# Attention's projections dealt out anew over 18 interleaved rounds, with new step counts and new yield points, in a three-block float32 kernel

## The chip, the core and the metric

One NeuronCore of a Trainium2 chip runs the whole program. The metric is device time in microseconds from start to end of the launch; before the change the median of three runs is 2845.41 us (2844.46 to 2849.97). The engines are PE (TensorE, matmuls), DVE (VectorE), ACT (ScalarE), POOL (GpSimd) and SP (SyncE, which only issues DMAs); each works through its own list of instructions in order.

## The reference, cut to what matters

Three residual blocks over x of 1024 tokens by 1024 features, all in float32. The change lies in the first block's stick-breaking attention and in the second block, whose two halves are an RWKV-7 time mix and a dilated window attention:

```python
def stick_breaking_attention(q, k, v):        # first block
    ...
    tail = lax.cumsum(log_one_minus, axis=3, reverse=True) - log_one_minus
    weights = masked_exp(causal, log_beta + tail)
    ...

def second_block(x, ...):
    xn = rms_norm(h, norm_w)
    p = jnp.einsum('bsd,dn->bsn', xn, w_in)                    # 1024 x 8320
    p_tm = p[..., :SHIFT_COLS]                                 # r, k, v, decay and rate columns
    p_tm = p_tm + (prev - p_tm) * mu_shift                     # prev: p_tm one token earlier
    y_rwkv = rwkv7_time_mix(p_tm, p[..., RWKV_GATE0:ATT0], ...)
    y_att = mixed_dilated_attention(p[..., ATT0:ATT_GATE0], p[..., ATT_GATE0:])
    h = h + jnp.einsum('bsm,md->bsd', jnp.concatenate([y_rwkv, y_att], axis=-1), w_out)
    return rms_norm(h, final_norm_w)

# rwkv7_time_mix, per token and head (16 heads of 64):
    sa = jnp.einsum('bhvk,bhk->bhv', state, av_t)
    state = state * w_t + sa * bv_t + v_t * k_t
    y_t = state @ r_t                                          # then a group norm, a bonus, a gate
```

## The kernel before, in words

Every projection is a dense product of float32 values split into a high and a low part (fp32r), so that each product of a 128x128 weight tile takes three matmuls (`mm3`, lines 308 to 312: high by high, low by high, high by low). A projection of 128 output features over 1024 tokens (`dense_gen`, line 314) is 2 halves x 8 contraction tiles = 16 steps of three matmuls over 512 columns, 48 matmuls in all, and yields after each step. `tok_gen` does the same for attention's values with 256 columns: also 16 yields, 96 matmuls. Dense products accumulate in the PSUM tiles called pd; their weights come by four 256 KB DMAs on SP, four casts on ACT (line 281) and four subtractions on DVE (line 282).

The order of the program is made by `interleave` (line 157). It is given Python generators, each with a stated number of steps n and a stretch (a, b) of the round, and always runs the one whose position a + (b - a) * done / n is smallest; a generator gives way wherever it yields. What it sets is the order in which instructions are written, and by it their rank: a scheduler below it then puts on each engine the first instruction in that order whose inputs it takes to be ready, so later dense matmuls already slip between the links of a chain.

The first block (`mixing1`) interleaves six rounds of projections with the mixing of the round before; `M1` holds the mixing's stated steps. Rounds 1 and 2 mix by `stick` (60 steps stated and made): per 128 queries, scores, two sigmoids on ACT, masks, a running product from the end (line 577) and a product (line 578) on DVE, then PE transposes of the result `be` (line 589) and the products with v.

The second block (`rwkv`, line 926) has 18 rounds over 16 units, a unit being two heads by 512 tokens. In round `it` it interleaves

- `rw_chain` of unit it-2: eight chunks of 64 tokens, each a chain cy (line 1169) -> R (copies, lines 1170 on DVE and 1171 on ACT) -> up (1174) -> SV (1175, 1176) -> sp (1178) -> the next state (1182), with A's product (1183) at its side; then the group norm of y (lines 1186 to 1197), transposes of y (1204) and the gate. It makes 11 + `GNY` steps, as stated;
- `rw_inverse` of unit it-1: 62 small DVE instructions, and round trips through DRAM on SP's queue;
- `rw_feat` of unit it: the decay (two tanh on ACT, a scan on DVE at line 1005, two exponentials on ACT at lines 1009 and 1010) and the products from it. 20 steps are stated, 16 made;
- dense work: `ATT[it]` of attention's 28 projection jobs (q, k, gate, and values for every other head pair), then `rw_dense`, the projections of a later unit. 32 steps are stated for `rw_dense` in rounds 0 to 15; it makes 32 in rounds 0 to 13, none in round 14 and 16 in round 15.

Jobs that `ATT` leaves over go into `attention`, as the first part of the filler `fill`, of which `AFILL[it]` steps run in attention's round `it`, beside loads of q and k (`at_load`, on ACT's queue for the first unit), scores (`at_scores`) and outputs (`at_out`). The residual's eight tiles r of 512 KB each are loaded on SP in attention's round 0.

Of the kernel before, what the change touches and what calls it, by code (L numbers as in the profile page):

```python
# [12 lines left out]
AF = mybir.ActivationFunctionType  # L13
ALU = mybir.AluOpType
# [158 lines left out]

ATT = [1, 2] * 3 + [1] * 10 + [3, 3]
G1 = [0, 5, 3, 5, 1, 7]
M1 = [60, 60, 46, 46, 78]
APLAN = [(0.0, 0.8), (0.0, 0.9), (0.0, 1.0)]
AFILL = [28, 20, 6] + [6] * 14
L3 = (0.2, 1.1)
WB = [(4,), (5, 3), (4,), (5,), (5,), (4, 3)]  # L180
MRB = 2
GNY = 4
TRM = (0.0, 0.8)
# [20 lines left out]
class Kern:  # L204
# [342 lines left out]
    def stick(self, pm, pr, q, k, v, y):  # L547

        nc = self.nc
        for i in range(NT):  # L550
# [10 lines left out]
            for h in range(2):  # L561
# [17 lines left out]
                bes.append(be)  # L579
                yield  # L580
            po = self.mm_ps()[:, :128]
            for g0 in range(0, i + 1, 4):
# [351 lines left out]
    def rwkv(self):  # L934
        nc, tc, I = self.nc, self.tc, self.I
        with tc.tile_pool(name="rw", bufs=1, reuse_waits="tile") as rw, self.psum(mx=2, iv=1, ch=1, cy=1):
# [15 lines left out]
            for it in range(18):  # L952
                gens = []
                if it >= 2:
                    gens.append((self.rw_chain(rw, U[it - 2]), 11 + GNY, *PLAN[0]))
                if 1 <= it <= 16:
                    gens.append((self.rw_inverse(rw, U[it - 1]), 37, *PLAN[1]))
                if it < 16:
                    gens.append((self.rw_feat(rw, U[it]), 20, *PLAN[2]))
                jobs = list(islice(att, ATT[it]))  # L960
                gens.append((chain(*jobs, self.rw_dense(rw, it)), 32 * (it < 16) + 16 * len(jobs), *PLAN[3]))
                interleave(gens)
# [20 lines left out]
    def rw_feat(self, rw, S):  # L983
# [20 lines left out]
        yield  # L1004
        V.tensor_tensor_scan(sg, self.c("cm"), sg, 0.0, ALU.mult, ALU.add)
        e1 = self.t(rw, [128, 8, 65], "E1")
        ei = ff("ei")
        nc.gpsimd.memset(e1[:, :, 0:1], 1.0)
        nc.scalar.activation(e1[:, :, 1:65], c8(sg), AF.Exp, scale=-cc)
        nc.scalar.activation(ei, sg, AF.Exp, scale=cc)  # L1010
        S["dc"] = dc = self.t(rw, [128, 8], "dc", bufs=3)
# [134 lines left out]
    def rw_chain(self, rw, S):  # L1146
# [16 lines left out]
        for c in range(8):  # L1163
# [8 lines left out]
            for n, s in enumerate((E, O)):  # L1172
                nc.scalar.activation(sd[s], sv[s, c, n], AF.Identity, scale=dc[s])  # L1173
            nc.tensor.matmul(up, xs[:, c], R, start=True, stop=True)
            V.tensor_copy(sv[E, c, 0], up[E])
            nc.scalar.copy(sv[O, c, 1], up[O])
            both = sv[:, c].rearrange("p n v -> p (n v)")
            nc.tensor.matmul(sp, M3[:, c].rearrange("p n k -> p (n k)"), both, start=True, stop=True)  # L1178
            for n, s in enumerate((E, O)):
# [12 lines left out]
        TT(c8(y), c8(y), bc(st[:, 0:8]), ALU.add)  # L1192
        nc.scalar.activation(sq, y, AF.Square)
        yield
        V.tensor_reduce(st[:, 8:16], c8(sq), AX.X, ALU.add)
# [53 lines left out]
    def attention(self):  # L1249
# [3 lines left out]
        with tc.tile_pool(name="po", bufs=1, reuse_waits="tile") as po:  # L1253
# [28 lines left out]
            with tc.tile_pool(name="at", bufs=1, reuse_waits="tile") as at, self.psum(**PB), \  # L1282
# [13 lines left out]
                for it in range(17):  # L1296
                    gens = [(residual(), 9, 0.1, 0.9)] if it == 0 else []
                    if it < 15:
                        gens.append((self.at_load(aqk, U[it + 1]), 4 + 2 * U[it + 1]["hf"], *ALP))
                    if it < 16:  # L1300
                        gens.append((self.at_scores(at, U[it]), 25, *APLAN[0]))
                    if it >= 1:
                        gens.append((self.at_out(at, U[it - 1]), 7 + 2 * U[it - 1]["hf"], *APLAN[1]))
                    if it == 9:
                        self.mact = macts[3] = self.act_half(1, 0)
                    if AFILL[it]:
                        gens.append((islice(fill, AFILL[it]), AFILL[it], *APLAN[2]))
                    interleave(gens)
# [446 lines left out]
```

## Time and profile before

| what | value |
| --- | --- |
| median of 3 runs | 2845.41 us (2844.46 to 2849.97) |
| the profiled execution: its own time | 2842.42 us |
| the profiled execution: span, first to last instruction | 2840.6 us |
| mean granted clock of TensorE, as a share of full speed | 0.986 |
| busy: PE, PEld (weight loads), DVE, ACT, POOL | 96%, 80%, 62%, 41%, 10% |
| rounds 1 to 17 of the RWKV part | about 1071 to 2005 us of the span |
| the stick rounds | about 70 to 410 us |

The profile's waits name whom an engine sat idle for. A view by stretches gives each engine's busy time and the granted clock in a window. Granted clock 1.00 is the upper of TensorE's two levels, 2.4 GHz, and 0.50 the lower, 1.2 GHz; a value between is a mix of both over the stretch. Matmuls are pipelined, so the busy time of one (0.39 us) is longer than its share of the stream.

### The profile page before, as it was taken

What the parts mean: (1) busy time and instruction counts of PE and PEld (TensorE: products, weight loads), DVE (VectorE), ACT (ScalarE), POOL (GpSimd) and SP (SyncE); (2) the same over time, 40 slices, a digit from 0 to 9 for tenths busy, and PEclk for the clock granted to TensorE, in tenths of its full rate; (3) what the DMA queues carried; (4) which work ended last, traced back from release to release, by engine and by line L of the source; (5) the groups of instructions that cost most, each with busy time, mean ns of one, the idle gap of its engine ahead of it and who ended that gap; (6) DMA issues with size and microseconds to landing.
All of it is one profiled execution on the core that took longest, in us unless ns stands there. A gap on an engine that the chain in (4) does not pass through costs nothing. (4 is left out here: it accounts for less than half of the span.)

```text
span 2840.6 us, 50116 instructions
## 1 busy us (share of the span) xinstructions
PE 2732.7 (96%) x18984; PEld 2277.3 (80%) x18984; DVE 1762.3 (62%) x4655; ACT 1174.7 (41%) x2808; POOL 275.5 (10%) x370
## 2 busy tenths in 40 slices
PE   9999999999998999999999999989999999999999
PEld 7778787777798787778877778768889989978887
DVE  4665533433867567787787877765466676644354
ACT  4433323223324324444445444444465666442232
POOL 0000000000213100010011100100011211000100
PEclk9999999999999999999999999989999999999999
DMA  3121111114753322222222222222754553331132
GB/s 124 45 68 45 56 65 38 57 57 148 226 191 115 98 85 66 72 74 69 78 66 79 69 72 75 68 66 73 209 181 143 165 161 109 132 118 66 48 121 97
DMA packets 215265, 276.63 MB, mean 97 GB/s; under 512 B 70112, under 2 KB 105712, under 8 KB 214896
## 3 DMA queue, kind: packets, MB, share of 16 engines
q1 hardware_dynamic: 187024, 220.99, 25.4%
q10 hardware_dynamic: 28000, 52.44, 5.1%
q8 instruction: 149, 2.44, 0.4%
q14 instruction: 92, 0.75, 0.1%
HBM read 213.58 MB, written 59.77 MB: 96 GB/s over the span
## 5 line engine op out<-in xcount | busy, mean ns | idle before, releaser
L310 PE MATMUL pd<-aH,wh 128*128 128x512 f32 (+1 forms) x1824 | 758.5, 416 | 12.4 <-ACT aH L305 5.9
L312 PE MATMUL pd<-aH,wl 128*128 128x512 f32 (+1 forms) x1824 | 735.1, 403 | 2.2 <-DVE wl L282 2.2
L311 PE MATMUL pd<-aL,wh 128*128 128x512 f32 (+1 forms) x1824 | 731.2, 401 | 0.0
L282 DVE TENSOR_TENSOR wl<-wraw,wh 128x512 fp32r<-128x512 f32 (+1 forms) x429 | 305.0, 716 | 303.1 <-ACT wh L281 293.5
L281 ACT CAST wh<-wraw 128x512 fp32r<-128x512 f32 (+1 forms) x429 | 260.4, 611 | 433.8 <-PE pd L311 214.3
L310 PEld LDWEIGHTS pd<-aH,wh 128*128 128x128 f32 (+1 forms) x1824 | 345.8, 190 | 85.2 <-issue 14.4
L312 PEld LDWEIGHTS pd<-aH,wl 128*128 128x128 f32 (+1 forms) x1824 | 345.3, 189 | 72.6 <-DVE wl L282 4.5
L311 PEld LDWEIGHTS pd<-aL,wh 128*128 128x128 f32 (+1 forms) x1824 | 346.5, 190 | 57.9 <-DVE aL L306 0.4
L310 PE MATMUL pd<-wh,aH 128*128 128x256 f32 x960 | 283.1, 296 | 2.7 <-ACT wh L281 2.2
L311 PE MATMUL pd<-wl,aH 128*128 128x256 f32 x960 | 273.7, 286 | 0.9 <-DVE wl L282 0.9
L312 PE MATMUL pd<-wh,aL 128*128 128x256 f32 x960 | 272.1, 286 | 1.4 <-DVE aL L306 1.2
L310 PEld LDWEIGHTS pd<-wh,aH 128*128 128x128 f32 x960 | 183.4, 192 | 7.7 <-ACT wh L281 3.4
L311 PEld LDWEIGHTS pd<-wl,aH 128*128 128x128 f32 x960 | 183.8, 192 | 4.1 <-DVE wl L282 1.8
L312 PEld LDWEIGHTS pd<-wh,aL 128*128 128x128 f32 x960 | 183.3, 192 | 2.7 <-DVE aL L306 2.3
L1447 ACT ACTIVATE S<-S,anm 128x256 f32<-128x256 f32 (+1 forms) x256 | 118.0, 463 | 22.5 <-DVE anm L1440 19.5
L1173 ACT ACTIVATE sd<-SV,dc 64x64 f32<-64x64 f32 x256 | 88.4, 345 | 83.6 <-DVE SV L1182 78.4
L1111 DVE TENSOR_TENSOR Xt<-At,X 128x60 f32<-128x60 f32 (+24 forms) x496 | 106.4, 214 | 11.1
L1113 DVE TENSOR_TENSOR X<-X,Xt 128x60 f32<-128x60 f32 (+24 forms) x496 | 104.7, 211 | 12.2
L1398 DVE CUSTOM_DVE_ANT_0 S<-sc,cf 128x256 f32<-128x256 f32 (+1 forms) x256 | 86.1, 377 | 31.3 <-PE sc L1395 21.7
L1394 PE MATMUL sc<-kk,qq 128*128 128x256 f32 (+1 forms) x256 | 90.5, 369 | 4.6 <-DVE kk L1369 3.6
L1169 PEld LDWEIGHTS cy<-SV,M 128*128 128x128 f32 x512 | 81.1, 193 | 16.2 <-DVE SV L1182 4.1
L1182 DVE SCALAR_TENSOR_TENSOR SV<-ch,dc,sd 64x64 f32<-64x64 f32 x240 | 67.9, 283 | 30.6 <-PE ch L1178 24.2
(376 smaller groups left out, 4857.2 us busy)
## 6 DMA issues: line engine op xcount, KB each, us to landing
wraw<-in_w2fm SPq DMA_DIRECT2D x122, 256.0 KB, 2.7
wraw<-in_w1fm SPq DMA_DIRECT2D x80, 256.0 KB, 2.6
qkr<-qkg SPq DMA_DIRECT2D x152, 128.0 KB, 2.8
wraw<-in_w2out SPq DMA_DIRECT2D x64, 256.0 KB, 3.4
sgd<-s ACTq DMA_DIRECT2D x48, 256.0 KB, 2.0
sgt<-sgd SPq DMA_DIRECT2D x48, 256.0 KB, 3.6
qkg<-ast ACTq DMA_DIRECT2D x42, 256.0 KB, 2.0
wraw<-in_w3fm SPq DMA_DIRECT2D x38, 256.0 KB, 2.6
```

What stands on the lines that cost most here:

```text
L281: nc.scalar.copy(h, raw)
L282: nc.vector.tensor_tensor(l, raw, h.bitcast(F32), ALU.subtract)
L310: mm(ps, lh, rh, start=start, stop=False)
L311: mm(ps, lh, rl, start=False, stop=False)
L312: mm(ps, ll, rh, start=False, stop=stop)
L1111: eng.tensor_tensor(tmp[:, :M, :n], At[:, j:j + 1, j + 1:32].to_broadcast([128, M, n]), X[:, :M, j:j + 1].to_broadcast([128, M, n]), ALU.mult)
L1113: eng.tensor_tensor(X[:, :M, j + 1:32], X[:, :M, j + 1:32], tmp[:, :M, :n], ALU.add)
L1169: nc.tensor.matmul(xy[:, c, n], M1[:, c, n], sv[:, c, n], start=c % 4 == 0 and n == 0, stop=False, skip_group_check=True)
L1173: nc.scalar.activation(sd[s], sv[s, c, n], AF.Identity, scale=dc[s])
L1394: mm(o, q, k, start=i == 0, stop=False, skip_group_check=True)
L1398: red = lambda o, x, mk, acc: V.tensor_tensor_reduce(o, x, mk, 1.0, -3e38, ALU.add, ALU.max, acc)
L1447: nc.scalar.activation(x, x, AF.Exp, bias=nm[:, n, h, t:t + 1], accum_out=l[:, n, h, t:t + 1])
```

## The change

Numbers that set the order change, four generators get more yield points, and the scan and the exponentials of `rw_feat` are done in two halves of 256 tokens. No other instruction is added or taken away.

- `ATT`: per round before 1 2 1 2 1 2 1 1 1 1 1 1 1 1 1 1 3 3, now 1 2 1 2 1 2 1 0 1 1 0 1 1 1 3 2 2 2. The sum falls from 25 to 24: one more job (48 matmuls) goes to attention's filler, and `AFILL` starts 34, 24, 12 in place of 28, 20, 6.
- The dense steps stated per round become those made (32 up to round 13, 0 in round 14, 16 in round 15). The chain is stated as 30 + `GNY` with `GNY` 8 and makes 28 + `GNY`; `rw_feat` is stated as 22 and makes 20.
- `stick` yields 1 + i // 3 times more before its transposes of query tile i, 15 times in all, so it makes 75 steps; `M1` still states 60.
- `ASTART`: the scores of attention's first unit are spread over 0.4 to 0.95 of their round in place of 0 to 0.8.

```diff
--- before.py
+++ after.py
@@ -171,15 +171,16 @@
             live.remove(x)
 
 
-ATT = [1, 2] * 3 + [1] * 10 + [3, 3]
+ATT = [1, 2] * 3 + [1, 0, 1, 1, 0, 1, 1, 1, 3, 2, 2, 2]
 G1 = [0, 5, 3, 5, 1, 7]
 M1 = [60, 60, 46, 46, 78]
+ASTART = (0.4, 0.95)
 APLAN = [(0.0, 0.8), (0.0, 0.9), (0.0, 1.0)]
-AFILL = [28, 20, 6] + [6] * 14
+AFILL = [34, 24, 12] + [6] * 14
 L3 = (0.2, 1.1)
 WB = [(4,), (5, 3), (4,), (5,), (5,), (4, 3)]
 MRB = 2
-GNY = 4
+GNY = 8
 TRM = (0.0, 0.8)
 YD = 0
 LNP = 4
@@ -577,6 +578,8 @@
                 nc.vector.tensor_tensor_scan(omr, omr, omr, 1.0, ALU.mult, ALU.min)
                 nc.vector.tensor_tensor(be[:, :W], be[:, :W], om[:, 1:W + 1], ALU.mult)
                 bes.append(be)
+                yield
+            for _ in range(1 + i // 3):
                 yield
             po = self.mm_ps()[:, :128]
             for g0 in range(0, i + 1, 4):
@@ -952,13 +955,13 @@
             for it in range(18):
                 gens = []
                 if it >= 2:
-                    gens.append((self.rw_chain(rw, U[it - 2]), 11 + GNY, *PLAN[0]))
+                    gens.append((self.rw_chain(rw, U[it - 2]), 30 + GNY, *PLAN[0]))
                 if 1 <= it <= 16:
                     gens.append((self.rw_inverse(rw, U[it - 1]), 37, *PLAN[1]))
                 if it < 16:
-                    gens.append((self.rw_feat(rw, U[it]), 20, *PLAN[2]))
+                    gens.append((self.rw_feat(rw, U[it]), 22, *PLAN[2]))
                 jobs = list(islice(att, ATT[it]))
-                gens.append((chain(*jobs, self.rw_dense(rw, it)), 32 * (it < 16) + 16 * len(jobs), *PLAN[3]))
+                gens.append((chain(*jobs, self.rw_dense(rw, it)), 32 * (it < 14) + 16 * (it == 15) + 16 * len(jobs), *PLAN[3]))
                 interleave(gens)
             self.late_jobs = list(att)
         self.rk_pool.__exit__(None, None, None)
@@ -1002,12 +1005,17 @@
         nc.scalar.activation(ta, aps, AF.Tanh, bias=self.ha0[:, p:p + 1], scale=0.5)
         nc.gpsimd.tensor_scalar(sg, sg, 0.5, 0.5, ALU.mult, ALU.add)
         yield
-        V.tensor_tensor_scan(sg, self.c("cm"), sg, 0.0, ALU.mult, ALU.add)
         e1 = self.t(rw, [128, 8, 65], "E1")
         ei = ff("ei")
         nc.gpsimd.memset(e1[:, :, 0:1], 1.0)
-        nc.scalar.activation(e1[:, :, 1:65], c8(sg), AF.Exp, scale=-cc)
-        nc.scalar.activation(ei, sg, AF.Exp, scale=cc)
+        halves = [(slice(256 * n, 256 * n + 256), slice(4 * n, 4 * n + 4)) for n in range(2)]
+        for tk, cs in halves:
+            V.tensor_tensor_scan(sg[:, tk], self.c("cm")[:, 0:256], sg[:, tk], 0.0, ALU.mult, ALU.add)
+            yield
+        for tk, cs in halves:
+            nc.scalar.activation(e1[:, cs, 1:65], c8(sg)[:, cs], AF.Exp, scale=-cc)
+            nc.scalar.activation(ei[:, tk], sg[:, tk], AF.Exp, scale=cc)
+            yield
         S["dc"] = dc = self.t(rw, [128, 8], "dc", bufs=3)
         nc.gpsimd.tensor_copy(dc, e1[:, :, 64])
         yield
@@ -1171,10 +1179,12 @@
             nc.scalar.copy(R[O], xy[O, c, 1])
             for n, s in enumerate((E, O)):
                 nc.scalar.activation(sd[s], sv[s, c, n], AF.Identity, scale=dc[s])
+            yield
             nc.tensor.matmul(up, xs[:, c], R, start=True, stop=True)
             V.tensor_copy(sv[E, c, 0], up[E])
             nc.scalar.copy(sv[O, c, 1], up[O])
             both = sv[:, c].rearrange("p n v -> p (n v)")
+            yield
             nc.tensor.matmul(sp, M3[:, c].rearrange("p n k -> p (n k)"), both, start=True, stop=True)
             for n, s in enumerate((E, O)):
                 if not (hf == 1 and c == 7):
@@ -1191,6 +1201,7 @@
         V.tensor_scalar(st[:, 0:8], st[:, 0:8], -1.0 / 64, None, ALU.mult)
         TT(c8(y), c8(y), bc(st[:, 0:8]), ALU.add)
         nc.scalar.activation(sq, y, AF.Square)
+        yield
         yield
         V.tensor_reduce(st[:, 8:16], c8(sq), AX.X, ALU.add)
         self.rsqrt(rw, st[:, 16:24], st[:, 8:16], 1.0 / 64, 64e-5)
@@ -1298,7 +1309,7 @@
                     if it < 15:
                         gens.append((self.at_load(aqk, U[it + 1]), 4 + 2 * U[it + 1]["hf"], *ALP))
                     if it < 16:
-                        gens.append((self.at_scores(at, U[it]), 25, *APLAN[0]))
+                        gens.append((self.at_scores(at, U[it]), 25, *(APLAN[0] if it else ASTART)))
                     if it >= 1:
                         gens.append((self.at_out(at, U[it - 1]), 7 + 2 * U[it - 1]["hf"], *APLAN[1]))
                     if it == 9:
```

Round 15 on PE: the last chunks of unit 13's chain. In the file before, cy, up, sp and A's product are L1169, L1174, L1178 and L1183, in the changed one L1177, L1183, L1188 and L1193; L1066 and now L1074 are products of `rw_feat`, L311 to L313 dense matmuls. Before:

```order
L1183 MATMUL cy_18936<-SV_1575_9416,A_18087 128x128
L1169 MATMUL cy_18936<-SV_1575_9416,M_3065_18085 128x64 x2
L1174 MATMUL ch_19275<-R_19278,XS_1573_9414 128x64
L1178 MATMUL ch_19276<-SV_1575_9416,M_3103_18343 128x128
L1183 MATMUL cy_18936<-SV_1575_9416,A_18087 128x128
L1169 MATMUL cy_18936<-SV_1575_9416,M_3065_18085 128x64 x2
L1174 MATMUL ch_19352<-R_19355,XS_1573_9414 128x64
L1178 MATMUL ch_19353<-SV_1575_9416,M_3103_18343 128x128
L1183 MATMUL cy_18936<-SV_1575_9416,A_18087 128x128
L1169 MATMUL cy_19478<-SV_1574_9415,M_3175_18718 128x64 x2
L1066 MATMUL mx_19299<-M_3261_19191,At_19192 128x128 x4
```

Now, in the last chunk of the same unit:

```order
L1177 MATMUL cy_18981<-SV_1575_9416,M_3039_17880 128x64 x2
L1074 MATMUL mx_19437<-M_3269_19286,At_19287 128x128 x4
L312 MATMUL pd_19406<-aL_1099_7118,wh_19247 128x512
L313 MATMUL pd_19406<-aH_1098_7117,wl_19248 128x512
L1074 MATMUL mx_19453<-M_3269_19286,At_19287 128x128 x2
L1183 MATMUL ch_19427<-R_19430,XS_1573_9414 128x64
L1074 MATMUL mx_19453<-M_3269_19286,At_19287 128x128 x2
L311 MATMUL pd_19406<-aH_1098_7117,wh_19247 128x512
L312 MATMUL pd_19406<-aL_1099_7118,wh_19247 128x512
L313 MATMUL pd_19406<-aH_1098_7117,wl_19248 128x512
L311 MATMUL pd_19406<-aH_1098_7117,wh_19247 128x512
L1188 MATMUL ch_19428<-SV_1575_9416,M_3065_18084 128x128
```

Before, three chunks run with nothing between their links, and the feature products come after them; now feature products and two to four dense matmuls stand between the links.

ACT in round 3, around the exponentials: E and ei are their outputs, R is the chain's copy. Before:

```order
L1001 ACTIVATE fs_11317<-mx_11284,hw_1504_9143 128x512
L1002 ACTIVATE ta_11318<-mx_11285,ha_1505_9145 128x512
L1009 ACTIVATE E_1899_11338<-fs_11317 128x8x64
L1171 COPY R_11296<-cy_11212 64x64
L1010 ACTIVATE ei_11339<-fs_11317 128x512
L1016 ACTIVATE fs_11378<-rkv_1654_9826,pf 128x512
L1176 COPY SV_1575_9416<-ch_11293 64x64
```

Now:

```order
L1004 ACTIVATE fs_11319<-mx_11289,hw_1504_9143 128x512
L1005 ACTIVATE ta_11320<-mx_11290,ha_1505_9145 128x512
L1181 ACTIVATE sd_11309<-SV_1575_9416,dc_10081 64x64 x2
L1016 ACTIVATE E_1899_11340<-fs_11319 128x4x64
L1017 ACTIVATE ei_11341<-fs_11319 128x256
L1016 ACTIVATE E_1899_11340<-fs_11319 128x4x64
L1017 ACTIVATE ei_11341<-fs_11319 128x256
L1179 COPY R_11310<-cy_11221 64x64
L1024 ACTIVATE fs_11461<-rkv_1653_9823,pf 128x512
```

R stood behind one whole exponential; here it stands behind four halves. In the 14 rounds that have feature and chain together it stands behind two halves in four, three in five and four in five.

SP at the start of attention: cf are constants, ag and vn gate and values of the first unit, r the residual's tiles, qkr raw q and k of the second unit. Before:

```order
L227 DMA cf_20582<-in_c 128x784
L1382 DMA ag_20591<-qkg 128x512
L1384 DMA vn_20592<-vd 128x4x128
L1293 DMA r_3473_20543<-hd 128x1024
L1293 DMA r_3474_20544<-hd 128x1024
L1415 DMA vn_20674<-vd 128x4x128
L1293 DMA r_3475_20545<-hd 128x1024
L1293 DMA r_3476_20546<-hd 128x1024
L1293 DMA r_3469_20539<-hd 128x1024
L1354 DMA qkr_20584<-qkg 64x512 x2
```

Now:

```order
L228 DMA cf_20560<-in_c 128x784
L1304 DMA r_3463_20521<-hd 128x1024
L1304 DMA r_3464_20522<-hd 128x1024
L1304 DMA r_3465_20523<-hd 128x1024
L1304 DMA r_3466_20524<-hd 128x1024
L1393 DMA ag_20646<-qkg 128x512
L1395 DMA vn_20647<-vd 128x4x128
L1304 DMA r_3459_20517<-hd 128x1024
L1304 DMA r_3460_20518<-hd 128x1024
L1365 DMA qkr_20562<-qkg 64x512 x2
L1365 DMA qkr_20602<-qkg 64x512 x2
```

Four of the eight r loads moved ahead of the first unit's gate and values, and six, no longer five, stand ahead of the second unit's q and k.

## Rows read from the trace of the kernel before

**Rows 1.** The page: busy time by engine; granted clock in 40 slices.
```profile
PE 2732.7 (96%) x18984; PEld 2277.3 (80%) x18984; DVE 1762.3 (62%) x4655; ACT 1174.7 (41%) x2808; POOL 275.5 (10%) x370
...
PEclk9999999999999999999999999989999999999999
```

**Rows 2.** Stretches of rounds; us, busy by engine, PEclk, DMA share, GB/s.
```profile
1674.50:1732.30 57.80, 55.34 (x356) 43.10 (x356) 44.85 (x141) 28.29 (x69) 6.86 (x11) 1.00 0.23 69
1800.00:1851.40 51.40, 47.96 (x320) 36.64 (x320) 42.88 (x126) 24.85 (x63) 7.00 (x12) 0.99 0.25 78
1851.40:1906.70 55.30, 43.83 (x274) 35.58 (x273) 42.59 (x133) 23.68 (x60) 3.73 (x5) 0.81 0.18 46
1906.70:1956.80 50.10, 48.85 (x297) 39.34 (x297) 28.59 (x112) 23.12 (x60) 2.68 (x3) 0.95 0.31 98
```

**Rows 3.** The same stretches, line 310 alone (one dense matmul in three).
```profile
1674.50:1732.30 57.80, 19.98 (x48) 9.11 (x48) 1.00 0.23 69
1800.00:1851.40 51.40, 15.05 (x35) 6.67 (x35) 0.99 0.25 78
1851.40:1906.70 55.30, 8.85 (x22) 4.25 (x21) 0.81 0.18 46
```

**Rows 4.** PE's timeline, first and last of 48 dense matmuls; start, duration in us.
```profile
1303.62 0.47 PE L310 MATMUL pd<-aH,wh 128*128 128x512 f32 x1
...
1314.38 0.39 PE L312 MATMUL pd<-aH,wl 128*128 128x512 f32 x1
```

**Rows 5.** PE's waits in 60:420, 1060:1800 (two rows), 2002:2100; total, times, longest.
```profile
PE mx L589 <- DVE be L578: 10.7, 11, 1.3
...
PE ch L1174 <- ACT R L1171: 14.9, 15, 1.7
PE ch L1204 <- DVE tt L1197: 2.2, 3, 1.2
...
PE sc L1394 <- DVE kk L1369: 3.6, 2, 2.3
```

**Rows 6.** PE's timeline in round 15; idle before and releaser in brackets.
```profile
1885.66 0.64 PE L1183 MATMUL cy<-SV,A 128*128 128x128 f32 x2
...
1899.66 0.90 PE L1204 MATMUL ch<-cf,tt 128*128 128x128 f32 x3 [2.57 <-DVE tt L1197]
```

**Rows 7.** Timelines of DVE and ACT in round 14, scan, exponential and R.
```profile
1806.80 1.22 DVE L1005 TENSOR_TENSOR_SCAN fs<-cf,fs 128x512 f32<-128x512 f32 x1
...
1808.05 0.63 ACT L1009 ACTIVATE E<-fs 128x512 f32<-128x512 f32 x1 [1.72 <-DVE fs L1005]
1808.71 0.21 ACT L1171 COPY R<-cy 64x64 f32<-64x64 f32 x1
```

**Rows 8.** ACT's groups by shape; busy, mean ns of one.
```profile
L1447 ACT ACTIVATE S<-S,anm 128x256 f32<-128x256 f32 x176 | 87.0, 496 | 12.4 <-DVE anm L1440 12.4
...
L1009 ACT ACTIVATE E<-fs 128x512 f32<-128x512 f32 x16 | 10.1, 632 | 21.4 <-DVE fs L1005 21.3
```

**Rows 9.** PE's timeline, a stick tile's last scores and its transposes.
```profile
174.92 0.63 PE L568 MATMUL mx<-f,q 128*128 128x512 f32 x2
...
181.11 0.95 PE L589 MATMUL mx<-cf,be 128*128 128x128 f32 x7 [1.31 <-DVE be L578]
```

**Rows 10.** PE's timeline in round 12, last product of the chain and y's transposes.
```profile
1715.23 0.39 PE L1183 MATMUL cy<-SV,A 128*128 128x128 f32 x2
...
1728.00 0.66 PE L1204 MATMUL ch<-cf,tt 128*128 128x128 f32 x4 [0.75 <-DVE tt L1197]
```

**Rows 11.** Stretches at the start of attention (as rows 2); landing of r's loads.
```profile
2010.00:2020.00 10.00, 8.13 (x36) 6.38 (x34) 0.96 (x2) 1.84 (x3) 0.00 (x0) 1.00 1.01 290
2020.00:2030.00 10.00, 8.30 (x36) 6.80 (x37) 4.39 (x14) 2.88 (x5) 0.00 (x0) 0.83 1.01 291
...
DMA to landing us min/median/max: 3.9/5.9/7.1
```

## The prediction, made before the changed kernel was run

> **What bounds the kernel now.** I read the page first: PE is busy for 96% of the span [rows 1], so no other engine is the bound as a whole, and as the change removes no matmul it can only win time in which PE stands still or runs slowly. The page's row of granted clock shows where to look, one slice under 0.9; a matmul's busy time is not its share of the stream, so I did not take the 96% for the limit. The second view is by stretches, cut where the RWKV rounds begin on PE (the transposes of v, line 1101). Round 12 is 57.8 us at clock 1.00; round 15 is 55.3 us with PE busy for only 43.8 of them and a granted clock of 0.81; round 16 has 0.95 [rows 2]. The third view counts dense work in them by line 310, one dense matmul in three: 48, then 35 in round 14 and 22 in round 15 [rows 3]. So round 15 is almost as long as round 12 with less than half of its dense work: the stated 32 steps that `rw_dense` does not make had used up the filler early. The last view is PE's waits by releaser: stick's transposes wait 10.7 us in 11 places, the chain's up product 14.9 us in 15, y's transposes 2.2 us, and attention's first scores 3.6 us [rows 5].
>
> **The change part by part.** A dense matmul costs 10.76 us / 47 = 0.229 us in the stream [rows 4].
>
> Round 15. Its rest beside dense work is 55.3 - 66 x 0.229 = 40.2 us; round 12's is 57.8 - 144 x 0.229 = 24.8 us [rows 2, 3]. The order now gives round 15 all 144 dense matmuls, placed between the links that stood bare. If its rest becomes that of round 12, the gain is **15.4 us**. What hides the chain is then this filler; without it the next to be late are y's transposes, which came 14.0 us after the chain's last product there, 2.57 us of it idle [rows 6].
>
> Round 14. Rest 51.4 - 105 x 0.229 = 27.4 us, so **2.6 us** to gain by the same step [rows 2, 3]. Round 16: half speed for 10% of 50.1 us makes work of 2.5 us cost 5; without the hole before it, **2.5 us** [rows 2].
>
> The light rounds. Rounds 7 and 10 lose a job each and have 105 and 107 dense matmuls in the new order. The nearest row is round 14 before, with 105: **-2.6 us each, -5.2** [rows 2, 3]. The bounds are nothing, if the new points of giving way cover it, and -15.4 each, if they go the way of round 15; I take round 14, whose count is the same.
>
> The group norm's tail. In round 12 y's transposes came 12.8 us after the last product and still waited 0.75 us [rows 10]. By counts from the new order at 0.229 us a dense and some 0.1 us a small matmul, an estimate, the work between the two is 6.0, 7.7 and 7.5 us in three rounds (7, 10 and 11) and 9.8 or more in the others with features, where the least was 9.2 before round 14. Beyond what the light rounds are charged I take **-3 us**; bounds 0 and -15, as three tails of 12.8 us would have it.
>
> The scan in halves. Before, the scan takes 1.22 us, E follows for 0.63 and R is done 0.21 after [rows 7], and up waits for it about 1 us a round. A half scan is an estimate of 0.61 us. A half exponential lies between half of 0.632 us and the 0.496 us of ACT's nearest shape of 256 columns [rows 8]; I take 0.40. Where R stands behind two halves it comes about 0.4 us sooner, behind three it comes at the same time, behind four 0.4 us later: nearly nothing over the 14 rounds. But the order now writes the previous chunk's sp and A and one dense matmul more behind the feature's first products and ahead of this up, some 0.45 us of work in most rounds: 14 x 0.45 = 6 us, of which I take **4**. The bounds are +14.9, every wait gone, and -6, 15 waits longer by 0.4. The Trainium skill ("VectorE: DVE Perf Modes", section on the TRN2 errata) says that operations from SBUF pay a fixed cost each on ScalarE and VectorE and advises tiles of at least 512 elements, which speaks against halves. Its formula gives an estimated 0.40 us for a half exponential, which fits between the rows; by that rule the halves cost ACT 0.17 us each, and the sum stays as it is because ACT is not the bound.
>
> Stick. In query tile 7 the second head's transposes start 6.2 us after the last scores, 1.31 us of it idle [rows 9]. Before, 12 to 15 dense matmuls (2.7 to 3.4 us) stood there; now 18 to 30 do (4.1 to 6.9 us) in tiles 0 to 6, which covers the waits. But 75 steps run against 60 stated, so the dense steps run out early: in tile 7 only 14 follow the last scores, and the last products get less between them. Of 10.7 us [rows 5] I leave about 6 standing or new: **+5**; bounds +10.7 and +2.
>
> Attention's start. One job moves here (48 x 0.229 = 11.0 us of PE work, four weight loads of 256 KB on SP, two stores on ACT's queue); PE's sum is unchanged. Of dense work after y's transposes there were 69 matmuls of 512 columns, 15.8 us; now 45 of these and 36 of 256 columns, an estimate of 14.6 us, precede the first scores, so these wait longer. The DMA engines are full there, share 1.01 and 290 GB/s [rows 11], and four r loads, 2.1 MB or 7.2 us at that rate, moved ahead. SP's waiting r loads also hold the gate and values queued behind them, which are needed only later. Against that stands more filler once the scores run. I take **-1 us**; bounds -15, those 7.2 us waited for at half speed, and +8, all waits and half speed gone.
>
> Nothing else costs: the added scan and exponentials lie beside PE's work, and 15 further idle points in stick and four more before y's transposes issue nothing. In rounds 14 and 15 the added jobs put eight weight loads each between the inverse's round trips on SP, as in rounds 2 to 6 before, at clock 1.00.
>
> **Sum.** 15.4 + 2.6 + 2.5 - 5.2 - 3 + 4 + 5 - 1 = 20.3 us off the profiled execution's 2842.4, that is 2822.1. The median of the runs lies 3.0 us above that execution (2845.4), so I predict **2825.1 us**.
>
> **The rivals.** *Light rounds become holes.* DVE is busy for 42.9 of round 14's 51.4 us and 44.9 of round 12's 57.8 [rows 2]; if rounds 7 and 10 fall into waiting and half speed as round 15 did, each loses 15.4 and not 2.6: 2825.1 + 25.6 = **2850.7**, no change. For: the cover of y's transposes falls to 6.0 and 7.7 us there. Against: round 14 with the same count kept clock 0.99. Chance 0.13.
>
> *The tail is slower than its cover in all rounds* (the slower side). Place: y's transposes, with everything behind them on PE. The covers counted from the new order for rounds 2 to 15 are 10.8, 14.8, 11.0, 14.8, 10.7, 6.0, 12.2, 12.8, 7.7, 7.5, 9.9, 9.8, 12.2 and 11.3 us. If the tail always needs the 14.0 us of round 15 [rows 6], they fall short by 46.1 in all; less 2.2 waited before [rows 5] and 8.2 charged above, that is 35.7: **2860.8**. At 13 us it is 2848.8, so it decides from some 13.2 us. For: the 12.8 us with a wait of round 12 [rows 10]. Against: only three such waits stand in 12 rounds, though the same count gives covers of 9.2 to 11.6 us in six of them. The Trainium skill ("TensorE: Matmul & The Clock Gate", section on HAM oscillation) describes waits that recur in each loop pass and halve the clock each time; the 0.81 of round 15 agrees [rows 2], and by that rule the price would rise further. Chance 0.07.
>
> *Attention's first scores wait for r.* The bound of -15 in place of -1: **2839.1**. Chance 0.10.
>
> *The halves don't free R* (the change does not do there what it says): -6 in place of +4, **2835.1**. Chance 0.08.
>
> **How the numbers follow.** My forecast has 0.62, within 2806 (all waits of up and stick gone, nothing lost in the light rounds) and about 2836. A measurement of this kernel tells about 0.2% from no change, here 5.7 us. Faster by more than that (below 2839.7): the forecast 0.62, the halves 0.08, half of the r rival 0.05 and 0.03 of a partial light-round loss, 0.78. Within 0.2%: the rest of the r rival 0.05, light rounds 0.07 and the tail's low end 0.01, 0.13. Slower: light rounds 0.03, the tail 0.06, 0.09. The range 2806 to 2843 leaves out the tail, 0.10 of the light rounds and about 0.03 below.
>
> **What would show it.** Right: round 15 at clock 1.00 and 57 us with 144 dense matmuls; waits of stick's transposes under 5 us in sum; up's waits still there, 8 to 14 us in sum; rounds 7 and 10 at 47 to 52 us. Wrong: granted clock under 0.95 in round 7 or 10, y's transposes waiting over 15 us in sum between rounds 2 and 15, or over 8 us ahead of attention's first scores.

## The result and the profile after

The changed kernel takes 2816.27 us in the median (2809.37 to 2818.79), the kernel before 2847.69 (2844.46 to 2849.99) beside it: ratio 0.9885, 95% interval 0.9867 to 0.9904. That is 1.15% faster, clear of the noise of the runs, inside the range (2806 to 2843) and 8.8 us below the forecast of 2825.1. The profiled execution of the changed kernel took 2815.63 us, its span is 2813.8; that is 26.8 us less span than before, where the sum of the prediction said 20.3.

The page of the changed kernel, busy time and granted clock, as [rows 1]:

```profile
PE 2719.9 (97%) x18984; PEld 2270.6 (81%) x18984; DVE 1748.2 (62%) x4671; ACT 1177.5 (42%) x2840; POOL 274.1 (10%) x370
...
PEclk9999999999999999999999999999999999999999
```

The slice under 0.9 is gone. Stretches of the changed kernel, cut as in [rows 2] at the transposes of v (now line 1109): rounds 15 and 16 (its first 50 us), then the light rounds 7 and 10, which have no job of attention:

```profile
1824.00:1879.80 55.80, 54.88 (x356) 43.80 (x355) 43.91 (x139) 27.65 (x69) 4.30 (x6) 1.00 0.29 86
1879.80:1929.80 50.00, 48.79 (x318) 38.68 (x318) 32.15 (x124) 24.99 (x69) 2.67 (x3) 1.00 0.28 86
1377.60:1425.40 47.80, 46.89 (x318) 36.27 (x317) 42.88 (x138) 24.34 (x64) 4.92 (x9) 1.00 0.21 60
1538.70:1586.90 48.20, 47.55 (x319) 37.08 (x318) 42.37 (x141) 24.50 (x65) 5.50 (x11) 1.00 0.22 62
```

The same, line 311 alone (one dense matmul in three, as [rows 3]), round 15 and the light rounds:

```profile
1824.00:1879.80 55.80, 20.20 (x48) 9.14 (x48) 1.00 0.29 86
...
1377.60:1425.40 47.80, 14.68 (x35) 6.64 (x35) 1.00 0.21 60
1538.70:1586.90 48.20, 15.35 (x36) 6.84 (x36) 1.00 0.22 62
```

Round 15 is as long as before (55.8 against 55.3 us) and does 144 dense matmuls in place of 66, at clock 1.00 in place of 0.81. The light rounds keep the full clock too.

PE's waits of the changed kernel; total, times, longest, as [rows 5]: stick (60:420); rounds 2 to 16 (1060:1960, two rows; 1071.6 us, which the table of the kernel before gives as the start of round 1, is that of round 2); around attention's start (1960:2100):

```profile
PE mx L592 <- DVE be L579: 4.6, 5, 1.1
...
PE ch L1215 <- DVE tt L1208: 10.5, 7, 2.1
PE ch L1183 <- ACT R L1179: 4.9, 10, 1.1
...
PE sc L1405 <- DVE kk L1380: 8.2, 2, 6.8
```

Stick's transposes (L592) wait 4.6 us where they waited 10.7. The rows of rounds 2 to 16 reach to 1960, those of before to 1800; to 1800 the up product (L1183) waits 4.6 us where it was 14.9, and y's transposes (L1215) went the other way, from 2.2 to 9.3. Over all of 1060:1960 up fell from 17.6 to 4.9 us and y's transposes rose from 7.8, round 15 among them, to 10.5; the rows of the kernel before there:

```profile
PE ch L1174 <- ACT R L1171: 17.6, 18, 1.7
PE ch L1204 <- DVE tt L1197: 7.8, 6, 2.6
```

One hole is new: 6.8 us ahead of attention's first scores, which now wait 8.2 us in two waits where they waited 3.6.

The sums of waits leave out matmuls that run slowly, and the lengths of rounds move with the jobs, so I add one measure that has neither fault. For every matmul I take the time from the start of the one before it on PE, less the median of that for its line and shape in the kernel before, and sum it over a stretch: **excess**, the time in which PE stood or went slowly, however much dense work was moved in or out. In us, one profile each:

```
                               before  after   e2   e5   e9  e10  e11  e12
opening and stick                27.1   20.1 28.4 20.7 19.1 16.5 20.6 16.3
first block's rest to round 1    94.9   95.9 95.0 95.8 96.4 93.0 95.4 95.0
rounds 2 to 6                    13.1    7.9 14.2 23.7 12.5  9.5  8.2  8.2
rounds 7 to 13                   20.6   22.5 25.4 26.9 23.6 11.4 16.6 16.7
rounds 14 to 16                  28.4    4.3  5.8  8.3  5.7 13.1  4.2  4.0
to attention's last scores        8.9   13.7  8.1 14.1  7.0 22.0  7.6 13.1
all behind                       12.8   14.8 13.1 13.1 11.9 13.1 12.4 10.9
```

Before to after: 24.1 us won in rounds 14 to 16, 7.0 in opening and stick (6.4 of it in stick), 5.2 in rounds 2 to 6; 1.9 lost in rounds 7 to 13, 4.8 in attention, 3.0 in the two other rows. That is 26.6 of the 26.8 us. How far one profile can be trusted is shown by kernels that give PE the same order in the rounds: the changed one, e3, e6, e7 and e8 lie between 29.7 and 32.7 us over rounds 2 to 13. The runs behind the names come now; each stands beside runs of the kernel before of its own, and the ratio is to those.

### The profile page after: what moved, and what is told of

The parts are those of the page before. It is cut to its first block, busy times and chain, and to the rows that moved or that the text cites. A ratio compares the mean times of both kernels' runs of the same rounds, so it can differ in the third digit from the quotient of the medians.

```text
span 2813.8 us, 50166 instructions
## 1 busy us (share of the span) xinstructions
PE 2719.9 (97%) x18984; PEld 2270.6 (81%) x18984; DVE 1748.2 (62%) x4671; ACT 1177.5 (42%) x2840; POOL 274.1 (10%) x370
## 4 chain that ended last, share of the span: by engine, by line
PE 43%; DVE 5%; ACT 3%; issue 3%; DMA 2%; POOL 1%; ACTq 0%; SPq 0%; DVEq 0%; POOLq 0%
PE pd L311 8%; PE pd L312 8%; PE pd L313 8%; PE po L1483 2%; PE mx L311 2%; PE mx L312 2%; PE tr L1493 2%; PE mx L313 2%; PE sc L1405 1%; PE sc L1406 1%; PE mx L1074 1%; PE cy L1177 1%; PE ch L1188 1%; DVE wl L283 1%; PE ch L1183 1%
## 5 line engine op out<-in xcount | busy, mean ns | idle before, releaser
L311 PE MATMUL pd<-aH,wh 128*128 128x512 f32 (+1 forms) x1824 | 760.9, 417 | 12.3 <-ACT aH L306 5.9
L313 PE MATMUL pd<-aH,wl 128*128 128x512 f32 (+1 forms) x1824 | 730.3, 401 | 2.2 <-DVE wl L283 2.2
L311 PEld LDWEIGHTS pd<-aH,wh 128*128 128x128 f32 (+1 forms) x1824 | 345.6, 189 | 76.0 <-issue 6.1
L313 PEld LDWEIGHTS pd<-aH,wl 128*128 128x128 f32 (+1 forms) x1824 | 344.7, 189 | 74.6 <-DVE wl L283 3.6
L312 PEld LDWEIGHTS pd<-aL,wh 128*128 128x128 f32 (+1 forms) x1824 | 346.0, 190 | 55.8 <-DVE aL L307 0.4
L311 PE MATMUL pd<-wh,aH 128*128 128x256 f32 x960 | 281.9, 295 | 5.0 <-ACT wh L282 2.6
L313 PE MATMUL pd<-wh,aL 128*128 128x256 f32 x960 | 271.1, 285 | 0.3 <-DVE aL L307 0.3
L311 PEld LDWEIGHTS pd<-wh,aH 128*128 128x128 f32 x960 | 182.8, 191 | 8.7 <-ACT wh L282 3.7
L313 PEld LDWEIGHTS pd<-wh,aL 128*128 128x128 f32 x960 | 183.0, 191 | 1.4 <-DVE aL L307 0.8
L1177 PEld LDWEIGHTS cy<-SV,M 128*128 128x128 f32 x512 | 81.5, 189 | 23.4 <-DVE SV L1192 11.3
L1406 PE MATMUL sc<-kk,ql 128*128 128x256 f32 (+1 forms) x256 | 86.9, 351 | 0.0
```

The source lines that it names most:

```text
L311: mm(ps, lh, rh, start=start, stop=False)
L312: mm(ps, lh, rl, start=False, stop=False)
L313: mm(ps, ll, rh, start=False, stop=stop)
L1177: nc.tensor.matmul(xy[:, c, n], M1[:, c, n], sv[:, c, n], start=c % 4 == 0 and n == 0, stop=False, skip_group_check=True)
L1406: mm(o, ql, k, start=False, stop=i == len(args) - 1, skip_group_check=True)
```

## Experiments

The theory: the dealing out wins rounds 14 to 16 and loses a little in the light rounds; the points of giving way win in stick and in the chain.

**e1, true step counts alone** (on the kernel before):

```diff
-                gens.append((chain(*jobs, self.rw_dense(rw, it)), 32 * (it < 16) + 16 * len(jobs), *PLAN[3]))
+                gens.append((chain(*jobs, self.rw_dense(rw, it)), 32 * (it < 14) + 16 * (it == 15) + 16 * len(jobs), *PLAN[3]))
```

> The kernel before with the true step counts of the dense generator alone (32 only up to round 13, 16 in round 15); the jobs stay where they were. Theory 1: round 15 needs both, steps spread over the round and more of them. The 66 dense matmuls now stand between the links, so its 20.2 us of PE time above the usual spacing falls to about 8 to 12 us, with waits left over: about 2838 us, granted clock in round 15 0.9 or more. Rival: the false count was the whole fault, round 15 keeps under 3 us above the usual spacing: about 2826 us. Other rival: it is the jobs alone, and nothing changes: 2845 to 2850 us.

Measured: 2844.58 us beside 2845.12, ratio 1.0004 (0.9991 to 1.0017): the last case, nothing. Round 15 of this kernel, all engines and then line 310 alone:

```profile
1849.10:1902.60 53.50, 40.92 (x274) 33.65 (x273) 39.22 (x129) 21.68 (x58) 3.29 (x4) 0.83 0.18 49
...
1849.10:1902.60 53.50, 9.25 (x22) 4.18 (x22) 0.83 0.18 49
```

Still 66 dense matmuls, still clock 0.83; the excess of the round falls from 20.2 to 17.3 us and round 16 pays that back with 3.4. The statement of 32 steps too many was not what left round 15 bare. With 66 dense matmuls in it the hole stays, by the false counts and by the true ones.

**e2, the whole dealing out without any point** (on the kernel before: `ATT`, counts, `ASTART`, `AFILL`).

> The kernel before with the whole dealing out (table of jobs, true counts, attention's start and fill), without any new point of giving way in stick, in the features and in the chain. Theory 1: rounds 14 to 16 gain their 24 us as in the changed kernel, the light rounds 7 and 10 lose about 4 us each for want of cover ahead of y's transposes, attention's start loses 5: about 2837 us, y's transposes waiting 10 us or more in sum in rounds 2 to 13. Rival: the light rounds are free by themselves, as rounds 7 and 10 were 0.8 and 1.9 us better in the changed kernel: about 2828 us. Other rival: without the points they fall into half speed: 2845 us or more.

Measured: 2831.58 us, ratio 0.9948 (0.9929 to 0.9967), so 13.5 us of the gain. Rounds 14 to 16 win 22.6 us, rounds 2 to 13 lose 5.9 (39.6 against 33.7). Attention's start loses nothing here (8.1 against 8.9), and the clock of the light rounds 7 and 10 is 0.99 and 1.00. Theory 1 held in rounds 14 to 16; the total lies between it and its rival, 5.4 us under the one and 3.6 over the other, since attention's start was free, and y's transposes wait 6.3 us in 6 places where 10 us or more were expected.

Two things belong to this. The run has jobs and true counts together; the jobs with the false counts were not run, so e1 and e2 show that the counts alone do nothing, and not that they are of no use beside the jobs. And `tok_gen` makes 8 x 8 x 3 = 192 matmuls of 256 columns for a job of values, not the 96 given at the start. Such a job moved from round 13 to round 14, which now has 288 dense matmuls, 192 of them of that kind.

**e3 and e8, stick's points taken out of the changed kernel.** The first edit took more than it said, the point after each head that was always there as well; the second is stick as before:

```diff
 # e8
                 bes.append(be)
-                yield
-            for _ in range(1 + i // 3):
                 yield
```

> The changed kernel without stick's new points of giving way. Theory 1: the 6.4 us won in stick go back, its transposes wait 9 to 11 us again in 10 or more places: about 2822.5 us. Rival: that stretch was better for other reasons, or what is lost there is won behind it: 2816 us, the same as the changed kernel.

> The changed kernel with stick as it was before (one point after each head, 60 steps run and 60 stated). The run without any point there showed more than was asked, since it also took the one that was always there. Theory 1: the points added are worth what the two profiles differ in there, 6.4 us: waits of stick's transposes 10 to 11 us in 11 places, about 2822.5 us. Rival: stick gains nothing that is not lost behind it: 2816 us.

Measured: e3 2825.67 us (ratio 0.9928, 0.9911 to 0.9945), with stick's transposes waiting 13.8 us in 18 places; e8 2823.04 us (0.9915, 0.9895 to 0.9934), with 10.7 us in 11 places as before and 28.0 us of excess in opening and stick where the changed kernel has 20.1. With no point, one and the new ones, the transposes wait 13.8, 10.7 and 4.6 us; the new points are worth some 7 us of the total (6.8 by the medians, 8.5 by the ratios).

**e4, whole scan and exponentials**, four points left at their place:

```diff
...
-        for tk, cs in halves:
-            V.tensor_tensor_scan(sg[:, tk], self.c("cm")[:, 0:256], sg[:, tk], 0.0, ALU.mult, ALU.add)
-            yield
+        V.tensor_tensor_scan(sg, self.c("cm"), sg, 0.0, ALU.mult, ALU.add)
+        yield
...
```

> The changed kernel with scan and exponentials whole again, and four points of giving way left at their place. Theory 1: the up product waits less because the chain gives way ahead of it, and not because R is freed by halves: its waits stay at 4 to 7 us in sum, about 2816 us. Rival: the halves free R: up's waits go back to 10 us or more, about 2823 us.

Measured: 2817.12 us, ratio 0.99 (0.9875 to 0.9925), no different from the changed kernel; up waits 7.0 us in 13 places. The halves take 2.1 us of waits from up (4.9 with them) and nothing that shows from the time.

**e5, e9 and e11: how the chain is spread.** Three edits of the changed kernel:

```diff
 # e5 and e9: the two points ahead of up and sp taken out
-            yield
             nc.tensor.matmul(up, xs[:, c], R, start=True, stop=True)
-            yield
             nc.tensor.matmul(sp, M3[:, c].rearrange("p n k -> p (n k)"), both, start=True, stop=True)
 # e5: stated 14 + GNY, GNY = 8    e9: stated 12 + GNY, GNY = 1
 # e11: the points stay, stated 30 + GNY
-GNY = 8
+GNY = 12
```

> The changed kernel without the two points at which the chain gives way ahead of its up and sp products (true count 16 lower). Theory 1: these points, and not the halves, took up's waits from 14.9 to 4.6 us: they go back to 10 us or more in 12 places or more, rounds 2 to 6 lose the 6 us won there: about 2823 us. Rival: the dealing out won it, since up waited only 10.3 us in 14 places with the dealing out alone, and the points add nothing: 2816 us, up's waits 5 to 10 us.

> The changed kernel without the two points ahead of up and sp, and with one idle point instead of eight ahead of y's transposes, stated 13: the chain's products are then spread over 0.61 of a round (8 of 13 steps), as in the changed kernel (24 of 38, 0.63). Without the points and with eight idle ones it was 8 of 22, 0.36, and 2832.6 us. Theory 2: it is the pace, how much dense work stands between one chunk and the next, that the stated counts set; 2816 to 2820 us, waits of the inverse's products and of M1's gone again. Rival (theory 1 as it was): the points themselves, which split the dense work of a chunk in three parts, are needed: up waits 10 us or more in sum, 2825 us or more.

> The changed kernel with twelve idle points instead of eight ahead of y's transposes, stated 42. Theory: the tail of the group norm is what still waits in the rounds (10.5 us in 7 places); four points more put about a tenth of a round more dense work ahead of the transposes: these waits fall under 4 us, up's and sp's rise by 2 to 4 since the products are drawn closer (24 of 42 steps): about 2813 us. Rival: what the tail wins the products lose in full, as where the pace was 0.36 of a round: 2816 to 2820 us.

Measured: e5 2832.62 us (0.9937, 0.9917 to 0.9958), e9 2814.82 (0.9897, 0.987 to 0.9925), e11 2803.05 (0.9854, 0.9831 to 0.9878). PE's waits in 1060:1960, of e5, e9 and e11 in turn:

```profile
PE iv L1140 <- DVE Xt L1137: 7.4, 6, 1.9
PE ch L1182 <- ACT R L1179: 3.4, 10, 0.4
PE mx L1074 <- DVE At L1064: 3.3, 4, 2.1
```

```profile
PE ch L1182 <- ACT R L1179: 10.4, 13, 1.5
PE ch L1213 <- DVE tt L1206: 5.7, 8, 1.1
```

```profile
PE ch L1183 <- ACT R L1179: 8.3, 10, 1.4
PE ch L1215 <- DVE tt L1208: 1.0, 2, 0.8
```

e5 came out slow, and not in the way expected: up waits less than ever, the inverse's products (L1140) and the M1 products (L1074) wait instead. (Its profile is of the longest of its five executions, 2839.56 us where the median is 2832.62, so its column of excess is too high rather than too low.) By stated steps the eight chunks are then done in 8 of 22, 0.36 of the round (before 8 of 15, 0.53; changed 24 of 38, 0.63); this share I call the pace. e9 gives the pace back (8 of 13, 0.61) and not the points: the time is that of the changed kernel, the waits for the inverse are gone, and up's return to 10.4 us. So both sides were partly right. The pace is what e5 had lost; the points do take up's waits away, 36.1 us of excess in rounds 2 to 13 without them and 30.4 with them, but 6.7 us less excess in attention hides that in e9's total. e11 puts work back ahead of y's transposes: they wait 1.0 us in place of 10.5, up 8.3 in place of 4.9, rounds 2 to 13 fall to 24.8 us, and the time lies under both cases expected. Between the last product of the chain and these transposes stood 5 of 15 steps before (0.33 of a round), 10 of 38 in the changed kernel (0.26) and 14 of 42 in e11 (0.33 again). So the changed step count had spread the products at the cost of the tail's cover, and e11 gives that back.

**e6 and e7: attention's start.** e6 has the old `AFILL` and scores from 0.0 to 0.8; e7:

```diff
-gens = [(residual(), 9, 0.1, 0.9)] if it == 0 else []
+gens = [(residual(), 9, 0.9, 1.5)] if it == 0 else []
```

> The changed kernel with attention's first unit from 0.0 to 0.8 and the fill of 28, 20 and 6 as before. Theory 1: the hole of 6.8 us ahead of the first scores comes from r's four loads, which here go behind more of the first unit's own loads; waits for kk fall to 2 to 5 us, but the late job then runs later and no time is won behind: 2812 to 2816 us. Rival: the hole is the shorter filler after the last transposes of y, and the old start, with less filler ahead of the scores, makes it longer: 2820 us or more.

> The changed kernel with the eight loads of r stated from 0.9 to 1.5 of attention's first round, so that they go behind the first unit's loads. Theory 1: the first scores wait for q and k, which share the DMA engines with four loads of r (2.1 MB); without these kk comes 4 us sooner, waits for kk under 3 us in sum, attention's first stretch 13.9 to about 9 us above the usual spacing: about 2811 us. Rival: q and k come late because of what ScalarE's own queue issues and when: the wait stays over 6 us, 2816 us.

Measured: e6 2822.79 us (0.9911, 0.989 to 0.9932), e7 2814.71 (0.9884, 0.9862 to 0.9907). e6 missed both ways: the hole stays (6.0 us) and is not longer, as the rival had it; and the loss is behind attention, 20.3 us of excess in place of 14.8, with 203 more dense matmuls left for after the last scores. e7 shortens the hole to 4.5 us and wins nothing that shows. What the rest of the hole waits for stands on ScalarE's timeline of the changed kernel (ACTq is an issue of DMAs on its queue):

```profile
1965.67 0.62 ACT L282 CAST wh<-wraw 128x512 fp32r<-128x512 f32 x1 [3.13 <-DMA wraw<-in_w2fm]
...
1966.54 3.39 ACTq L1365 DMA_DIRECT2D qkr<-qkg  x4
...
1975.15 0.62 ACT L1369 CAST qq<-qkr 128x512 fp32r<-128x512 f32 x1 [4.58 <-DMA qkr<-qkg]
```

The first unit's loads are issued only behind two casts, which wait 3.13 us for a late job's weights, and then take until 1975.15. With r out of the way (e7) the same wait of the cast qq is 2.64 us, from an issue at 1962.21 to 1968.07. So r costs about 2.3 us of the 6.8.

For the rest the order on ScalarE's queue was not changed by an edit of its own, but two runs from above differ in it. e2 and e9 have the same jobs, the same start of attention and four loads of r ahead of the first unit's gate as well, and their first scores wait hardly more than before:

```profile
PE sc L1395 <- DVE kk L1370: 2.4, 1, 2.4
PE sc L1403 <- DVE kk L1378: 2.1, 1, 2.1
```

On their ScalarE the issue stands behind two casts of this job and not four, and by the profile neither of the two waits for weights. From y's last transposes to the cast kk it takes 17.2 and 17.4 us there, 17.2 in the kernel before and 20.6 in the changed kernel. So the new hole came neither with the dealing out nor with r's place alone, but with the order on ScalarE that the chain's new steps leave at the end of round 17.

**e10, no light rounds, and 75 stated steps in stick** (far apart, read by stretch):

```diff
-ATT = [1, 2] * 3 + [1, 0, 1, 1, 0, 1, 1, 1, 3, 2, 2, 2]
+ATT = [1, 2] * 3 + [1, 1, 1, 1, 1, 1, 1, 1, 2, 2, 2, 1]
...
-M1 = [60, 60, 46, 46, 78]
+M1 = [75, 75, 46, 46, 78]
```

> The changed kernel with two edits in stretches that lie far apart: no light rounds (one job in each of rounds 6 to 13, two in 14 to 16, one in 17), and stick's stated steps 75, as many as run. To be read by stretch. Jobs: by the forecast's price the light rounds cost 5.2 + 3 us, which come back in rounds 7 to 11; rounds 14 and 15 have two jobs where they had three and two, and by the run with the true counts alone (17.3 us above the usual spacing with one job) round 15 keeps its cover, round 14 loses 2 us or less: together 5 us won. Rival: light rounds cost nothing, rounds 7 to 13 stay within 2 us of the changed kernel and 14 to 16 lose up to 5. Stick: dense work that reaches the last tiles covers the 4.6 us that still wait there: 2 to 4 us won; rival: it is spread thinner, the earlier tiles wait, none won. In sum 2808 us, by the rivals 2821 us.

Measured: 2817.32 us (0.9899, 0.9876 to 0.9922). Rounds 7 to 13 win 11.1 us: light rounds have a price, a third above the forecast's 8.2. No wait of y's transposes is left in rounds 7 to 12, where the changed kernel has one in each. But rounds 14 to 16 lose 8.8 and attention 8.3, more than expected. Stick wins 3.6; its waits for `be` fall from 4.6 to 0.2 us.

**e12, both winners**, `GNY` 12 and `M1` 75:

> The changed kernel with the two edits that won, twelve idle points ahead of y's transposes and 75 stated steps in stick. The stretches lie apart. Theory: both gains add, 13 us from the tail's points and 4 to 5 us from stick: about 2798 us. Rival: the 13 us were in part a good meeting of loads at attention's start (6 of them lie there), which another order of the dense work ahead undoes: about 2804 us.

Measured: 2805.86 us (0.9862, 0.9844 to 0.988), no better than e11. The profile has stick's 4.3 us (16.3 against 20.6), but attention's stretch is back at 13.1 us where e11 had 7.6, although on PE, ACT and DVE the two kernels have the same instructions in the same order from the end of stick on. So some 5 us there differ from one profile to the next, and the rival held in its number, not in its reason. Twelve idle points are better than eight in two kernels: rounds 2 to 13 have 24.8 and 24.9 us of excess, 5.6 below the changed kernel. How much of the rest of e11's gain (13 us by the medians, 9 by the ratios) is luck of that kind stays open.

## Why the prediction was right, and which terms were mis-sized

**Rounds 14 to 16**, 15.4 + 2.6 + 2.5 = 20.5: measured 24.1. The working held: round 15 at clock 1.00 with 144 dense matmuls, 55.8 us for the 57 forecast. But one sentence ahead of it is wrong, that the stated 32 steps "had used up the filler early": with them corrected alone round 15 keeps its hole (e1). The gain came when the jobs moved; the counts alone bring nothing.

**Light rounds and tail**, -5.2 and -3: the price was right in size, 8.2 forecast: beside a kernel without light rounds it is 11.1 us (e10), in the dealing out alone 5.9 over rounds 2 to 13 (e2). y's transposes, named as next to be late, wait 9.3 us in place of 2.2 up to 1800, under the 15 set as the mark. The place was right in part: they wait once in each of rounds 7 to 12, not only in 7, 10 and 11, whose cover was counted as short. That the smaller share of steps at the tail (0.26 of a round for 0.33) has a part in this is shown by e11.

**The halves and up's wait**, +4: this is the mis-sized term, and its reason was wrong too. From e2 to the changed kernel rounds 2 to 13 fall from 39.6 to 30.4 us, so all that was added there is worth about 9. I had looked for it in the halves, which bring nothing that shows (e4), and in one dense matmul more ahead of up. The larger part is the two points ahead of up and sp, which share the dense work out inside a chunk: with the pace and without them (e9) these rounds have 36.1 us, and up waits 10.4 us as it did in e2 (10.3). The other 3.5 us are the pace, the features' points and the tail's together; no run parts these, and as e9 has a shorter tail too, the split is rough. So up's waits, forecast at 8 to 14 us, fell below that to 4.6.

**Stick**, +5: 6.4 in the profile, about 7 in the runs (e8). That the dense steps run out early at 75 against 60 was right too: with 75 stated, 3.6 to 3.8 us more (e10, e12).

**Attention's start**, -1: -4.8, inside its bounds. But by the prediction's own marks this was wrong: over 8 us of waits ahead of attention's first scores was a sign of it, and by the sum that gave 3.6 before they wait 8.2. The rival of r was right in its place, the hole ahead of the first scores, and wrong in the main cause: r is 2.3 us of it (e7), and with the same loads of r the first scores of e2 and e9 wait 2.4 and 2.1 us.

**The rivals.** Light rounds as holes: no, clock 1.00 in both. The tail slower than its cover in all rounds: no, seven waits of at most 2.1 us. The halves that don't free R: no, with whole exponentials up waits 2.1 us more and not less (e4); but the time does not show it.

**The sum.** 3.6 us too little for rounds 14 to 16, some 5 for the chain's points and pace, about 2 for stick and a light-round price 2 too high, against 3.8 us too little charged for attention and 3 us of slower rest; that is the 6.5 us between 20.3 and 26.8 to within 1. So the total came nearer than its terms: misses of some 12.6 us one way and 6.8 the other partly cancelled, which is luck. The lower end of the range, 2806, is also off its own words: it holds up's waits and the light rounds, and with stick's waits, which it names, it would be 2800.3.

## What to carry to other kernels

Where one engine is fed by several generators, look at the stretch with the least filler and count the filler, before doubting where it is put: true counts alone moved nothing (e1), and with three jobs more in rounds 14 and 15 as well the stretch won 23 us (e2). When a chain gets new points of giving way, its stated count changes the share of the round in which its links are spread; two kernels here that differ in that share and in the tail's differ by 11 us by the ratios and 18 by the medians (e5 and e9), so an experiment on such points must hold the pace. And what is taken from one wait is to be sought in the next: four idle points at the tail that the spread chain had left bare won another 5.6 us in the rounds (e11).

## What the runs showed of the hardware

For the scan and the exponential here, halving costs a fixed part per instruction. The half scan takes 0.686 us where the whole took 1.22 [rows 7], more than the 0.61 estimated, so two halves cost 0.15 us more; the half exponentials take 0.418 and 0.402 us where the whole took 0.63. The prediction's estimate of 0.40 by the Trainium skill ("VectorE: DVE Perf Modes", section on the TRN2 errata) agrees with this. The extra 0.2 us on ACT for each exponential and 0.15 on DVE came to nothing that shows in the time (2816.27 us in halves, 2817.12 whole).

The clock of TensorE shows what a hole costs beyond itself. Stretches of the changed kernel, the hole ahead of attention's first scores and the 11 us behind it:

```profile
1971.90:1978.90 7.00, 0.20 (x1) 0.00 (x0) 1.38 (x2) 1.23 (x2) 0.00 (x0) 0.77 0.83 222
1978.90:1990.00 11.10, 9.67 (x42) 8.24 (x42) 4.68 (x19) 2.45 (x4) 0.00 (x0) 0.84 0.91 239
```

The granted clock falls to its lower level within the hole and is still there for a part of the work behind it. That this stretch gave 13.7, 7.6 and 13.1 us of excess in the changed kernel, e11 and e12, the last two in the same order of instructions, was not expected; where such a hole stands, a single profile is no measure to better than some 5 us.
